# The later adaLN modulation of a streaming Conformer layer: sums over slab rows on ScalarE and GpSimd, turned by transposes, in place of column-group products

## The chip, the cores and the metric

The kernel runs on one core of a Trainium2 chip. A core has five engines with instruction queues of their own: TensorE (PE in the profile, its weight loads PEld), VectorE (DVE), ScalarE (ACT), GpSimd (POOL) and SyncE (SP), which here only issues DMAs. Each engine works through its queue in order and waits on semaphores for the others. TensorE writes to PSUM; GpSimd can work in SBUF only. The metric is the device time of one execution in microseconds, the median of several runs.

## What is computed

One layer of a streaming encoder, for a prompt of 2048 rows and a sample of 64 rows (`T` = 2112 rows in all), width 1024, in float32. The change is in its first lines, the modulation by the conditioning vector `c`:

```python
mod = jax.nn.silu(c) @ p['w_ada'] + p['b_ada']
sh1, sc1, gt1, sh2, sc2, gt2 = [m[:, None, :] for m in jnp.split(mod, 6, axis=-1)]
h = rms_norm(x, p['norm1_g']) * (1 + sc1) + sh1
z = h @ p['w_in']          # convolution pair, q, k, v, two gates
...
x = x + gt1 * (merged @ p['w_o'])
h2 = rms_norm(x, p['norm2_g']) * (1 + sc2) + sh2
gate, up = jnp.split(h2 @ p['w_ffn_in'], 2, axis=-1)
x = x + gt2 * ((jax.nn.silu(gate) * up) @ p['w_ffn_out'])
```

`c` is one row of 1024 for the prompt and one for the sample, `w_ada` is 1024 x 6144. So the modulation is a product of two rows with a matrix of 24 MB, and it gives six vectors of 1024 for each of the two. The first two, `sh1` and `sc1`, are needed at once; `sh2`, `sc2`, `gt1` and `gt2`, the later modulation, are needed only in the second phase, behind the attention.

## The kernel before

**Phases.** The first phase goes over four blocks of rows (`PBLOCKS`, 576 + 3 x 512) and, in each, over the stages of `ORDER`: q, 0, k, 1, v, 2, 3, g. The stages q, k and v are projections (`qkv`), the stages 0 to 3 one quarter each of the convolution input (`glu`), the stage g the 16 tiles of gates. Between the matmuls of these stages run the attention, the convolution and the norms. The second phase, over `CBLOCKS`, has the two mixers' output projections and the FFN. Large products are made of three matmuls, with each operand split into a high and a low float32r part; the split of a weight is a ScalarE copy (`whi`) and a subtraction (`wlo`).

**The order of the work** is written by a planner while the program is built. Every engine is wrapped in a `Meter` (L88), which adds the estimated time of each instruction to that engine's load in `Stream.load` (L183): a matmul of 512 columns 213 ns, a ScalarE pass 220 + 0.83 n ns, a GpSimd operation 60 + 2.25 n ns. After each trio of matmuls `spend` (L212) calls `tick` if 500 ns of planned TensorE time have gone by; it calls the functions that are due and lets each `Lane` make one step or several of its generators (`pump`, L145). A generator yields the planned time from which it may go on, `stream.when(engine)` being the end of that engine's planned load less 200 ns (`LAG`). `PE_LAG` is 400 ns and `TURN_LAG` 2500 ns. `drain` (L166) runs a lane's generators to their ends at once. The matmuls keep the order in which they are written out (`manual_schedule`, L1686); the queues of the other engines are ordered by the compiler's scheduler from data dependences and that order.

**The later modulation.** `MOD_HALVES` (L561) lists its eight halves: for each of the four vectors (`c6` = 3, 4, 2, 5) two halves of 512 columns. A half is four slabs of `w_ada`, each 256 rows x 512 columns as a tile of 128 partitions x 2 x 512 (tag `wmod`, 4 buffers of 512 KB). `Slabs` (L235) loads them through SP's queue: a slab's `done` (L259) makes its buffer free when TensorE has passed, and the next slab's load is issued from there. `mod_steps` (L901) makes one half at the end of each stage in `MODS` (L562): `mod_sums` (L855) multiplies four slabs with the columns of `silu(c)` in `cl`, padded to 32, in four column groups of TensorE at a time (`tile_position`), 16 products a half; `mod_rows` copies the result to SBUF (tile `R`); `mod_columns` (L876), 2.5 us later by the plan, adds the groups up and turns rows into columns by two products with the constant `sel`, and VectorE adds the bias. At the end the gates' vectors are transposed and stored to `gt_d`. 

**Around it.** `attend` (L1551) runs a head of attention: scores (`sc`), maximum on VectorE, exponential on ScalarE, transposes (`ptp`) and the product with v (`po`). `convolve` (L1274) is VectorE's filler: 31 taps a quarter, each `y = u * w + y` over 512 columns in SBUF (`y<-u,wd,y`). `conv_norm` (L1296) has the LayerNorm sums, added up on GpSimd and finished by a product with `ones` (tile `pm`). `temp` (L783) gives one of seven scratch tiles of 128 x 512. `ps_g` has five PSUM banks. From block 2's stage g on the `wmod` buffers serve the attention's q and k (L1445).

Of the kernel before, what the change touches and what calls it, by code (L numbers as in the profile page):

```python
# [8 lines left out]
F32 = mybir.dt.float32  # L9
F32R = mybir.dt.float32r  # L10
AF = mybir.ActivationFunctionType
ALU = mybir.AluOpType
AX = mybir.AxisListType
# [3 lines left out]
P = 128  # L17
D = 1024
KT = 8
# [24 lines left out]
PE_LAG = 400.0  # L44
TURN_LAG = 2500.0
# [513 lines left out]


MOD_HALVES = [(c6, half) for c6 in (3, 4, 2, 5) for half in range(2)]  # L561
MODS = {at: 1 for at in ((1, 0), (1, 1), (1, 2), (1, "g"), (2, 0), (2, 1), (2, 2), (2, 3))}  # L562

ORDER = [(b, st) for b in range(4) for st in ("q", 0, "k", 1, "v", 2, 3, "g")]

# [23 lines left out]
def mod_order():  # L589
    for ct in range(0, KT, 2):  # L590
        yield from (("mod", c6, ct // 2, h, 0) for c6 in (0, 1) for h in range(2))
    yield from (("mod", *half, i) for half in MOD_HALVES for i in range(4))
# [30 lines left out]
def streaming_layer(ctx: ExitStack, tc: tile.TileContext, I, O):  # L623
    nc = tc.nc
    stream = Stream()
    pe, dve, act, gps = (
        Meter(e, n, stream) for e, n in ((nc.tensor, "pe"), (nc.vector, "dve"), (nc.scalar, "act"), (nc.gpsimd, "pool"))
    )
# [28 lines left out]
    ident = const.tile([P, P], F32, name="ident")  # L657
# [8 lines left out]
    A1 = const.tile([P, KT, 2], F32, name="A1")  # L666
    B1 = const.tile([P, KT, 2], F32, name="B1")
    A2 = const.tile([P, KT, 2], F32, name="A2")
    B2 = const.tile([P, KT, 2], F32, name="B2")
    cols = const.tile([P, 76], F32, name="cols")  # L670
    gates_c = const.tile([P, 2, 2, KT], F32, name="gates_c")
# [6 lines left out]
    g1, g2 = cols[:, 0:8], cols[:, 8:16]  # L678
    bdw, lng, lnb = cols[:, 16:20], cols[:, 20:24], cols[:, 24:28]
    b_ada = cols[:, 28:76]  # L680
# [95 lines left out]
    ps_g = p1.enter_context(tc.tile_pool(name="ps_g", bufs=5, space=PSUM))  # L776
    ps_a = p1.enter_context(tc.tile_pool(name="ps_a", bufs=1, space=PSUM))
    wk = p1.enter_context(tc.tile_pool(name="wk", bufs=1))
    cl = wk.tile([P, KT, 32], F32, name="cl")
# [3 lines left out]
    def temp(name, shape=(P, 512)):  # L783
        return wk.tile(list(shape), F32, tag="t", name=name, bufs=NT)
# [70 lines left out]
    def mod_sums(pa, keys):  # L855


        for i, key in enumerate(keys):
            w = M.get(key)
            a, b = w.shape[1:]  # L860
            for j in range(4):

                k, c = divmod(j * 2 * P, b)
                pe.matmul(
                    pa[32 * j : 32 * j + 32], cl[:, a * i + k], w[:, k, c : c + 2 * P], start=i == 0,
                    stop=i == len(keys) - 1, tile_position=(0, 32 * j),
                )
            M.done()

    def mod_rows(pa):  # L870
        R = temp("R", pa.shape)
        stream.after("dve", "pe")
        dve.tensor_copy(R, pa)
        return R

    def mod_columns(pc, R, c6, ct, nh):  # L876


        pc = pc.rearrange("p (e n) -> p e n", e=2)
        for e in range(2):  # L880
            pe.matmul(pc[:, e], R[:, e * P : e * P + P], sel, start=True, stop=True)
        stream.after("dve", "pe")
        pc = pc[:, :, 2 * (nh - 1) : 2 * (2 * nh - 1)].rearrange("p e (h s) -> p e h s", h=nh)
        cs = slice(ct, ct + 2 * nh)

        def place(a):
            return a[:, cs].rearrange("p (h e) s -> p e h s", e=2)

        def wide(a):
            return a.rearrange("p (h e) -> p e h", e=2).unsqueeze(3).to_broadcast([P, 2, nh, 2])  # L890

        bias = wide(b_ada[:, 8 * c6 + ct : 8 * c6 + ct + 2 * nh])
        gates_of = lambda i: gates_c[:, i].rearrange("p s k -> p k s")
        out = place({0: B1, 1: A1, 3: B2, 4: A2}[c6] if c6 not in (2, 5) else gates_of((2, 5).index(c6)))
        dve.tensor_tensor(out, pc, bias, ALU.add)
        if c6 in (1, 4):
            dve.tensor_tensor(out, out, wide({1: g1, 4: g2}[c6][:, cs]), ALU.mult)
        elif c6 in (2, 5):
            dve.tensor_scalar(out, out, {2: 0.25, 5: 0.5}[c6], None, ALU.mult)

    def mod_steps():  # L901
        for c6, half in MOD_HALVES:
            pa = ps_g.tile([P, 512], F32, tag="gp", name="pa")
            mod_sums(pa[:, : 2 * P], [("mod", c6, half, i) for i in range(4)])
            R = mod_rows(pa[:, : 2 * P])
            stream.at(
                stream.when("dve") + TURN_LAG, lambda pa=pa, R=R, c6=c6, half=half: mod_columns(pa[:, 2 * P :], R, c6, 4 * half, 2)
            )
            yield
        stream.flush()  # L910
        pt = ps_g.tile([P, 512], F32, tag="gp", name="pt")
        pe.transpose(pt[:32, :P], gates_c.rearrange("p c s k -> p (c s k)"), ident)
        row = temp("row")
        dve.tensor_copy(row[:32, :P], pt[:32, :P])
        nc.sync.dma_start(gt_d.rearrange("c s (k n) -> (c s k) n", n=P), row[:32, :P])
        yield

    def first_rows():
        places = ((wa, "x", 3), (wa, "x", 3), (wa, "x", 3), (wk, "kk", 1), (wk, "q2", 1))
# [748 lines left out]
    norm_lane, work = Lane({}, wide=NORM_W), Lane({}, wide=5)  # L1668
    attn = Lane(ATTN, ATTN_NS, wide=2, young=True)
    conv, tail = Lane({"dve": CONV_ROOM}, burst=4), Lane({})  # L1670
    stream.lanes = [norm_lane, work, attn, tail, conv]

    hh = wk.tile([P, KT, QB + SMP], F32R, tag="hh", name="hh")
    hl = wk.tile([P, KT, QB + SMP], F32R, tag="hl", name="hl")
# [4 lines left out]
    M = Slabs(nc.sync, nc.scalar, wa, stream, list(mod_order()), source, 4)  # L1679
# [5 lines left out]
    ordered = ExitStack()  # L1685
    ordered.enter_context(tc.manual_schedule(engines={mybir.EngineType.PE}))  # L1686
    norm_lane.add(cached_kv())
    mods = mod_steps()
    norms = {}
    for b, stage in ORDER:  # L1690
        lo, hi = PBLOCKS[b]
        if stage == "q":
            free, ahead = {"columns": 0}, {}
            if b + 1 < len(PBLOCKS):
                ahead = {t: norm_tile(hi, t, free) for t, _ in token_tiles(*PBLOCKS[b + 1])}
        if stage == "q" and b == 0:
            pass
        elif stage in ("q", "k", "v"):
            qkv(b, "qkv".index(stage), norms)
            if stage == "k":  # L1700
                work.wide = 3
            if stage == "v":

                def heads(b=b):
                    work.drain()
                    stream.flush()
                    attention(b)
                    if b == 3:
                        attn.burst, attn.spacing = 2, 0.0

                stream.at(stream.load["pe"] + HEADS_NS, heads)
        elif stage == "g":
            spare["open"] = b >= 2 and ("wide" if b == len(PBLOCKS) - 1 else "narrow")
            for g in gates(b, free):
                if g == SIDE_G - 4 and b == len(PBLOCKS) - 1:
                    spare["open"] = False
                if g == NORM_G:
                    to_load += list(ahead)
                    for _ in range(3):
                        load_ahead()  # L1720
                    for gen in ahead.values():
                        norm_lane.add(gen)
                if g == SIDE_G and b == len(PBLOCKS) - 1:
                    work.drain()
                    conv.drain()
                    while spare["heads"] and now["scored"] < spare["heads"][-1]:
                        attn.push()
                    stream.flush()
                    side.close()
                    wc = ctx.enter_context(tc.tile_pool(name="wc", bufs=1, side="right"))  # L1730
                    cs = tile_chunks(*CBLOCKS[0])[0]
                    src = load_mixed(*cs, 0)
                    first_gates = gate_columns(*cs, 0)
            norms = ahead
        else:
            if b == 0 and stage == 1:
                bias_rows()
            if stage == 0:
                conv.drain()
                tail.drain()  # L1740
                y = wk.tile([P, 4, YW], F32, tag="y", name="y")
            conv.add(convolve(glu(b, stage), y, stage, b))
            if stage == 3:
                if b == 0:
                    tail.add(conv_norm(y, 0, SMP, 0))
                    tail.add(conv_norm(y, SMP + HIST, QB, SMP))
                else:
                    tail.add(conv_norm(y, 0, QB, lo, b == len(PBLOCKS) - 1))
        for _ in range(MODS.get((b, stage), 0)):
            next(mods)  # L1750
    next(mods)
    attn.drain()
    conv.drain()
    tail.drain()
# [6 lines left out]
    ps_g = ctx.enter_context(tc.tile_pool(name="ps_c", bufs=4, space=PSUM))  # L1761
    wk = ctx.enter_context(tc.tile_pool(name="wk2", bufs=1))
    work = Lane({}, 600.0)
# [182 lines left out]
    for s, (lo, hi) in enumerate(CBLOCKS):  # L1946
        tiles = token_tiles(lo, hi)
        half = (hi - lo) // 2
        gt1, groups, hs = {}, [], None
        chunks = tile_chunks(lo, hi)  # L1950
        for i, (c0, c1) in enumerate(chunks):
# [30 lines left out]
            ws = {}  # L1982
# [385 lines left out]
        last = last_rows(s)  # L2368
# [14 lines left out]
        ws = [W.get(("fo", f)) for f in last]  # L2383
# [40 lines left out]
```

## Time and profile before

Three runs took 2940.25, 2942.64 and 2944.25 us, median 2942.64. The profile is of one execution, whose span from the first to the last instruction is 2938.6 us; it gives no other time of that execution.

| Engine | busy us | share of the span | instructions |
|---|---|---|---|
| span | 2938.6 | | 44831 |
| PE | 2887.0 | 98% | 16193 |
| PEld | 2584.9 | 88% | 16193 |
| DVE | 2059.1 | 70% | 3650 |
| ACT | 1362.6 | 46% | 2453 |
| POOL | 1167.1 | 40% | 753 |

All lines of engine work bear L105, the line of the wrapper that records them, so instructions are told apart by their tiles. A row of the timeline has the start in us from the span's start, the duration in us, engine, line, operation, output<-inputs, partitions x elements, the count where several are merged, and in brackets the idle time ahead of it with what ended it. Matmuls overlap in the pipeline: what one costs is the distance from its start to the next one's, not its duration. A row of groups has the count, then the busy time in us and the mean ns of one, then the idle time just before them. A row of the tile view has the shortest, median and longest duration in ns and the first and last start. A row of a table by stretches has from:to and the length, then for each engine the busy us and the number of its instructions, then the granted TensorE clock, the DMA engines' share and GB/s.

### The profile page before, as it was taken

What the parts mean: (1) busy time and instruction counts of PE and PEld (TensorE: products, weight loads), DVE (VectorE), ACT (ScalarE), POOL (GpSimd) and SP (SyncE); (2) the same over time, 40 slices, a digit from 0 to 9 for tenths busy, and PEclk for the clock granted to TensorE, in tenths of its full rate; (3) what the DMA queues carried; (4) which work ended last, traced back from release to release, by engine and by line L of the source; (5) the groups of instructions that cost most, each with busy time, mean ns of one, the idle gap of its engine ahead of it and who ended that gap; (6) DMA issues with size and microseconds to landing.
All of it is one profiled execution on the core that took longest, in us unless ns stands there. A gap on an engine that the chain in (4) does not pass through costs nothing.

```text
span 2938.6 us, 44831 instructions
## 1 busy us (share of the span) xinstructions
PE 2887.0 (98%) x16193; PEld 2584.9 (88%) x16193; DVE 2059.1 (70%) x3650; ACT 1362.6 (46%) x2453; POOL 1167.1 (40%) x753
## 2 busy tenths in 40 slices
PE   7999999999999999999999999999999999999999
PEld 5899777888888888888999998999999999999998
DVE  5897798668967876577777756666667557566666
ACT  3346543661564266563444345444444345444442
POOL 1201310111011003554566452366567742465667
PEclk9999999999999999999999999999999999999999
DMA  9989899978996997984444975333333965333333
GB/s 322 317 296 312 280 291 306 302 243 307 285 294 196 316 269 228 291 299 157 144 144 146 294 260 199 97 122 94 115 115 104 346 220 179 97 103 106 115 107 127
DMA packets 467067, 628.04 MB, mean 214 GB/s; under 512 B 36196, under 2 KB 314584, under 8 KB 466845
## 3 DMA queue, kind: packets, MB, share of 16 engines
q1 hardware_dynamic: 452944, 606.11, 64.1%
q10 hardware_dynamic: 13901, 19.08, 1.9%
q8 instruction: 127, 2.08, 0.3%
q14 instruction: 95, 0.78, 0.1%
HBM read 476.53 MB, written 148.54 MB: 213 GB/s over the span
## 4 chain that ended last, share of the span: by engine, by line
PE 47%; DVE 2%; ACT 1%; issue 1%; DMA 1%; POOL 0%; ACTq 0%; POOLq 0%; DVEq 0%
PE ps L105 28%; PE pd L105 14%; PE pw L105 5%; ACT whi L105 0%; DVE wlo L105 0%; DMA wst<-in_w_ffn_in 0%; DVE pw L105 0%; DVE ps L105 0%; DVE t L105 0%; POOL ws L105 0%; DMA tg<-g_d 0%; DVE acc L105 0%; DVE sums L105 0%; PE pt L105 0%; ACT xn L105 0%
## 5 line engine op out<-in xcount | busy, mean ns | idle before, releaser
L105 PE MATMUL ps<-t,whi 128*128 128x384 f32 (+1 forms) x2112 | 501.9, 322 | 2.7 <-ACT u L105 0.8
L105 POOL TENSOR_TENSOR wlo<-wst,whi 128x1024 fp32r<-128x1024 f32 (+1 forms) x159 | 364.1, 2302 | 215.3 <-ACT whi L105 215.2
L105 ACT ACTIVATE whi<-wst 128x1024 fp32r<-128x1024 f32 (+1 forms) x265 | 258.3, 979 | 318.8 <-PE ps L105 134.9
L105 PE MATMUL ps<-b,whi 128*128 128x384 f32 (+1 forms) x1584 | 380.4, 325 | 6.5 <-DVE v L105 2.1
L105 PEld LDWEIGHTS ps<-t,whi 128*128 128x128 f32 x2112 | 367.7, 188 | 10.2 <-ACT u L105 3.4
L105 DVE SCALAR_TENSOR_TENSOR y<-u,wd,y 128x512 f32<-128x512 f32 (+1 forms) x480 | 370.0, 774 | 8.2
L105 PE MATMUL ps<-hh,whi 128*128 128x512 f32 (+2 forms) x992 | 362.0, 365 | 0.1
L105 DVE TENSOR_TENSOR acc<-acc,pd 128x512 f32<-128x512 f32 x482 | 322.2, 685 | 47.9 <-PE pd L105 45.3
L105 PE MATMUL ps<-hh,wlo 128*128 128x512 f32 (+2 forms) x992 | 344.6, 347 | 0.0
L105 PE MATMUL ps<-hl,whi 128*128 128x512 f32 (+2 forms) x992 | 344.0, 347 | 0.0
L105 PE MATMUL ps<-t,wlo 128*128 128x384 f32 (+1 forms) x1056 | 338.2, 321 | 0.0
L105 PE MATMUL pd<-whi,hid 128*128 128x512 f32 x912 | 297.4, 391 | 0.5 <-DVE hid L105 0.3
L105 PEld LDWEIGHTS ps<-b,whi 128*128 128x128 f32 x1584 | 276.8, 188 | 14.8 <-DVE v L105 3.2
L105 ACT ACTIVATE pr<-pr,sm 128x640 f32<-128x640 f32 (+3 forms) x272 | 202.2, 749 | 133.3 <-DVE sm L105 130.9
L105 PE MATMUL ps<-b,wlo 128*128 128x384 f32 (+1 forms) x792 | 256.0, 323 | 0.0
L105 POOL TENSOR_TENSOR r<-t,mhalf 128x1 f32<-128x1 f32 (+2 forms) x68 | 82.8, 1225 | 408.0 <-DVE t L105 355.1
L105 DVE TENSOR_TENSOR wlo<-wst,whi 128x1024 fp32r<-128x1024 f32 (+1 forms) x106 | 135.3, 1280 | 101.6 <-ACT whi L105 100.1
L105 PEld LDWEIGHTS ps<-hh,wlo 128*128 128x128 f32 x992 | 186.3, 188 | 22.7
L105 PEld LDWEIGHTS pd<-whi,hid 128*128 128x128 f32 x912 | 171.1, 188 | 36.9 <-DVE acc L105 1.2
L105 PEld LDWEIGHTS ps<-hh,whi 128*128 128x128 f32 x992 | 186.7, 188 | 17.7 <-issue 2.5
L105 PEld LDWEIGHTS ps<-hl,whi 128*128 128x128 f32 x992 | 187.1, 189 | 14.7 <-issue 1.7
L105 PEld LDWEIGHTS ps<-t,wlo 128*128 128x128 f32 x1056 | 198.1, 188 | 0.8
(233 smaller groups left out, 6309.7 us busy)
## 6 DMA issues: line engine op xcount, KB each, us to landing
whi<-w_din_h SPq DMA_DIRECT2D x72, 512.0 KB, 6.8
wlo<-w_din_l SPq DMA_DIRECT2D x72, 512.0 KB, 6.9
wst<-sum_d SPq DMA_DIRECT2D x131, 256.0 KB, 2.9
wfo<-in_w_ffn_out SPq DMA_DIRECT2D x64, 512.0 KB, 4.0
wmod<-in_w_ada SPq DMA_DIRECT2D x46, 512.0 KB, 9.1
sum_d<-ws SPq DMA_DIRECT2D x88, 256.0 KB, 2.3
wst<-in_w_ffn_in SPq DMA_DIRECT2D x85, 256.0 KB, 3.2
wst<-in_w_in SPq DMA_DIRECT2D x40, 512.0 KB, 6.1
```

Of the source, the lines that this page charges most:

```text
L105: self.last = f(*args, **kw)
```

## The change

The eight halves are no longer multiplied on TensorE. For each of the eight groups of 128 rows in a half (`k`), ScalarE scales the slab's rows by `silu(c)` of the prompt into a scratch tile and by `silu(c)` of the sample in place, each partition with its own factor. GpSimd adds these up over `k`, the sums standing in the first slab's own buffer. What remains is a sum over 128 partitions: TensorE transposes the two sums of 128 x 512 in four squares each, and VectorE adds each square up along its rows (`tensor_reduce`), which gives the columns that the bias, scale and factor are applied to as before. All four slabs are released together at the end of a half.

The halves are generators in a lane of their own, the last in the list. Half i is added at the end of stage `MODS[i]`, beginning one entry earlier than before, at (0,"g") instead of (1,0); ahead of each addition the lane is drained, and once more at (2,3). `mod_columns` keeps the cases of the first two vectors only; `sel`, `cl` and `mod_sums` stay for these.

```diff
-MODS = {at: 1 for at in ((1, 0), (1, 1), (1, 2), (1, "g"), (2, 0), (2, 1), (2, 2), (2, 3))}
+MODS = [(0, "g"), (1, 0), (1, 1), (1, 2), (1, "g"), (2, 0), (2, 1), (2, 2)]
...
+    def mod_sum(c6, half, last):
+        ws = [M.get(("mod", c6, half, i)) for i in range(4)]
+        first = temp("first")
+        accs = [ws[0][:, 1], ws[0][:, 0]]
+        for k in range(KT):
+            w = ws[k // 2][:, k % 2]
+            t = temp("term") if k else first
+            act.activation(t, w, AF.Copy, scale=cl[:, k, 0:1])
+            act.activation(w, w, AF.Copy, scale=cl[:, k, 1:2])
+            if k:
+                stream.after("pool", "act")
+                gps.tensor_tensor(accs[1], accs[1], w, ALU.add)
+                gps.tensor_tensor(accs[0], first if k == 1 else accs[0], t, ALU.add)
+            yield stream.when("pool")
+        yield stream.when("pool") + PE_LAG
+        total = wk.tile([P, 2, 4], F32, tag="total", name="total", bufs=2)
+        for s in range(2):
+            pt = ps_g.tile([P, 4, P], F32, tag="gp", name="pt")
+            for j in range(4):
+                pe.transpose(pt[:, j], accs[s][:, j * P : j * P + P], ident)
+            stream.after("dve", "pe")
+            dve.tensor_reduce(total[:, s], pt, AX.X, ALU.add)
+        for _ in ws:
+            M.done()
...
+        dve.tensor_tensor(out, total, wide(b_ada[:, 8 * c6 + 4 * half : 8 * c6 + 4 * half + 4]), ALU.add)
+        if c6 == 4:
+            dve.tensor_tensor(out, out, wide(g2[:, cs]), ALU.mult)
         elif c6 in (2, 5):
             dve.tensor_scalar(out, out, {2: 0.25, 5: 0.5}[c6], None, ALU.mult)
-
-    def mod_steps():
-        for c6, half in MOD_HALVES:
-            pa = ps_g.tile([P, 512], F32, tag="gp", name="pa")
-            mod_sums(pa[:, : 2 * P], [("mod", c6, half, i) for i in range(4)])
-            R = mod_rows(pa[:, : 2 * P])
-            stream.at(
-                stream.when("dve") + TURN_LAG, lambda pa=pa, R=R, c6=c6, half=half: mod_columns(pa[:, 2 * P :], R, c6, 4 * half, 2)
-            )
-            yield
-        stream.flush()
+        if not last:
+            return
+        yield stream.when("dve") + PE_LAG
         pt = ps_g.tile([P, 512], F32, tag="gp", name="pt")
         pe.transpose(pt[:32, :P], gates_c.rearrange("p c s k -> p (c s k)"), ident)
...
-    stream.lanes = [norm_lane, work, attn, tail, conv]
+    mods = Lane({})
+    stream.lanes = [norm_lane, work, attn, tail, conv, mods]
...
-        for _ in range(MODS.get((b, stage), 0)):
-            next(mods)
-    next(mods)
+        if (b, stage) in MODS:
+            mods.drain()
+            i = MODS.index((b, stage))
+            mods.add(mod_sum(*MOD_HALVES[i], i + 1 == len(MODS)))
+        elif (b, stage) == (2, 3):
+            mods.drain()
```

More of the change, by code (lines that the diff above doesn't have):

```diff
@@ L892, in mod_columns @@
         bias = wide(b_ada[:, 8 * c6 + ct : 8 * c6 + ct + 2 * nh])
-        gates_of = lambda i: gates_c[:, i].rearrange("p s k -> p k s")
-        out = place({0: B1, 1: A1, 3: B2, 4: A2}[c6] if c6 not in (2, 5) else gates_of((2, 5).index(c6)))
+        out = place((B1, A1)[c6])
         dve.tensor_tensor(out, pc, bias, ALU.add)
-        if c6 in (1, 4):
-            dve.tensor_tensor(out, out, wide({1: g1, 4: g2}[c6][:, cs]), ALU.mult)
+        if c6:
+            dve.tensor_tensor(out, out, wide(g1[:, cs]), ALU.mult)
@@ new lines, in mod_sum @@
+    def mod_sum(c6, half, last):
[22 more added lines that the diff above has]
+            M.done()
+        cs = slice(4 * half, 4 * half + 4)
+        wide = lambda a: a.unsqueeze(1).to_broadcast([P, 2, 4])
+        if c6 in (2, 5):
+            out = gates_c[:, (2, 5).index(c6), :, cs]
+        else:
+            out = {3: B2, 4: A2}[c6][:, cs].rearrange("p k s -> p s k")
+        dve.tensor_tensor(out, total, wide(b_ada[:, 8 * c6 + 4 * half : 8 * c6 + 4 * half + 4]), ALU.add)
+        if c6 == 4:
+            dve.tensor_tensor(out, out, wide(g2[:, cs]), ALU.mult)
@@ L915, in mod_steps @@
         nc.sync.dma_start(gt_d.rearrange("c s (k n) -> (c s k) n", n=P), row[:32, :P])
-        yield
     def first_rows():
@@ L1687, in streaming_layer @@
     norm_lane.add(cached_kv())
-    mods = mod_steps()
     norms = {}
```

## The prediction

> **What bounds the kernel now.** I read the page's busy shares first, then its chain, then TensorE's timeline around the work that goes.
>
> ```profile
> PE 2887.0 (98%) x16193; PEld 2584.9 (88%) x16193; DVE 2059.1 (70%) x3650; ACT 1362.6 (46%) x2453; POOL 1167.1 (40%) x753
> PE 47%; DVE 2%; ACT 1%; issue 1%; DMA 1%; POOL 0%; ACTq 0%; POOLq 0%; DVEq 0%
> ```
>
> TensorE (PE) is busy 98% and the chain is nearly all PE. So a microsecond taken off PE's own list counts, and so does any wait put into it: PE's order is fixed by the planner, and what stands behind a waiting instruction waits too. The spare time of the other engines is worth something only where PE needn't wait for them.
>
> **PE's part.** The later products are 8 halves of 32 records (tile view, from 200 us on; first and last start are in the row); a half costs what PE's start-to-start times show:
>
> ```profile
> L105 PE MATMUL pa<-wmod,cl x256: 379/379/404, 356.6 to 747.9; 128*32 128x256 f32 x128
> ```
> ```profile
> 731.72 1.93 PE L105 MATMUL pa<-wmod,cl 128*32 128x256 f32 x32
> 733.58 0.50 PE L105 MATMUL ps<-hh,whi 128*128 128x512 f32 x1
> 733.92 0.40 PE L105 MATMUL ps<-hl,whi 128*128 128x512 f32 x1
> 734.15 0.39 PE L105 MATMUL ps<-hh,wlo 128*128 128x512 f32 x1
> ...
> 737.11 0.60 PE L105 MATMUL pa<-sel,R 128*128 128x128 f32 x4
> 737.47 0.48 PE L105 MATMUL ps<-hh,whi 128*128 128x512 f32 x1
> ```
> ```profile
> 618.22 0.60 PE L105 MATMUL pt<-ident,x_t 128*128 128x128 f32 x4
> 618.57 0.47 PE L105 MATMUL ps<-whi,hh 128*128 128x512 f32 x1
> 618.88 0.39 PE L105 MATMUL ps<-wlo,hh 128*128 128x512 f32 x1
> ```
>
> Products: 733.58 - 731.72 = 1.86, and the next matmul takes 0.34 instead of 0.23: 1.97 us. The two products with `sel`: 737.47 - 737.11 = 0.36, and about 0.09 behind them. Removed: 8 x 2.42 = 19.4 us. Added are 8 transposes a half; four take 618.57 - 618.22 = 0.35, with 0.08 behind a group: 8 x 0.78 = 6.2 us. PE's list gets 13.2 us shorter. The gates' last transpose is in both.
>
> **What is added elsewhere**, by the nearest forms (mean ns behind the busy time):
>
> ```profile
> L105 ACT ACTIVATE junk<-x_t 128x512 f32<-128x512 f32 x24 | 14.9, 623 | 3.1 <-DMA x_t<-in_x_prompt 3.0
> L105 POOL TENSOR_TENSOR s<-s,ln 128x512 f32<-128x512 f32 x12 | 15.9, 1324 | 32.3 <-ACT ln L105 32.2
> L105 DVE TENSOR_REDUCE ssq<-sq 128x8 f32<-128x512 f32 x32 | 21.6, 678 | 8.0 <-ACT sq L105 7.8
> ```
>
> A half is 16 ScalarE passes (16 x 0.62 = 10.0 us), 14 GpSimd adds in one dependent row (14 x 1.32 = 18.5 us) and two reductions (1.4 us; a 0.42 us copy goes). Eight halves: 80 us ScalarE, 148 us GpSimd. As busy time that disappears, both engines being under half full. What matters is the 20 us from a half's first pass to its last add, where that must be over, and whom it holds up.
>
> **The last half.** Where the stages end:
>
> ```profile
> 313.15 0.39 PE L105 MATMUL ps<-whi,hh 128*128 128x512 f32 x1
> ```
> ```profile
> 454.36 1.93 PE L105 MATMUL pa<-wmod,cl 128*32 128x256 f32 x32
> ```
> ```profile
> 696.53 1.93 PE L105 MATMUL pa<-wmod,cl 128*32 128x256 f32 x32
> ```
> ```profile
> 746.36 1.93 PE L105 MATMUL pa<-wmod,cl 128*32 128x256 f32 x32
> ```
>
> A half now starts where its predecessor's products stood (the first at the end of (0,"g"), 313) and must be over at the next entry. The last starts at the end of (2,2), 731.72, and is drained at (2,3), 746.36: 14.6 us for a row that takes 20. Its slabs aren't there at once either. The planner spaces a step by two passes (2 x 645 ns), two adds (2 x 1212) less 400 of lags, and the next tick: some 3.6 us, so 27 us for a half, 29 in PE's real time (planned 213 ns a matmul, 228 in the rows). Half 6, from 696.5, thus ends near 726, and only then are the last four slabs asked for:
>
> ```profile
> 734.42 2.11 SPq L249 DMA_DIRECT2D wmod<-in_w_ada  x4
> ```
> ```profile
> 365.80 2.28 SPq L249 DMA_DIRECT2D wmod<-in_w_ada  x4
> ```
> ```profile
> wmod<-in_w_ada SPq DMA_DIRECT2D x46, 512.0 KB, 9.1
> ```
>
> SP reaches them 2.7 us (734.42 after 731.72) to 9.2 us (365.80 after 356.6) behind the matmuls that free them, and they take 9.1 to land: about 738. Two passes and 14 adds later it is 758; PE has stood since 746.4, 11.5 us. Then the gates' transpose waits for reductions, bias and scale on DVE, behind a convolution tap or two: 2.5 us. Low bound, slabs there at 731.7: 5 + 1 = 6 us. High bound, each add taking turns with a tap (next part): 14 x (1.32 + 0.67) = 28, so 767, 21 + 3 = 24 us. I take 15, near the first working. Nothing covers this: everything PE has next stands behind it.
>
> The transposes of the other seven halves are placed 0.4 us behind the planned last add. The nearest case, the LayerNorm sums that wait for GpSimd with the same lag, hardly waits:
>
> ```profile
> PE pm L105 <- DVE h L105: 0.4, 1, 0.4
> ```
>
> Between 0 and 2 us each; I take 0.4, 3 us in all.
>
> **DVE against GpSimd.** Both read SBUF. Overlaps in the timelines, GpSimd rows first:
>
> ```profile
> 545.26 4.85 POOL L105 TENSOR_TENSOR y<-y,s 128x512 f32<-128x512 f32 x4 [13.44 <-DVE sm L105]
> ```
> ```profile
> 547.45 1.71 DVE L105 TENSOR_SCALAR y<-y,cols 128x512 f32<-128x512 f32 x1 [1.65 <-ACT ln L105]
> 549.19 1.46 DVE L105 SCALAR_TENSOR_TENSOR ln<-ln,y 128x512 f32<-128x512 f32 x1
> ```
> ```profile
> 1164.19 8.00 POOL L105 TENSOR_TENSOR wlo<-wst,whi 128x1024 fp32r<-128x1024 f32 x3 [11.07 <-ACT whi L105]
> ```
> ```profile
> 1164.66 5.29 DVE L105 TENSOR_TENSOR part_l<-ln,part_h 128x512 fp32r<-128x512 f32 x2 [0.51 <-ACT part_h L105]
> ```
> ```profile
> L105 DVE SCALAR_TENSOR_TENSOR y<-u,wd,y 128x512 f32<-128x512 f32 x360 | 268.6, 750 | 6.3
> ```
>
> Two subtractions that take about 0.7 us elsewhere took 5.29 beside three long GpSimd ones: the engines took turns. The 1.46 stands against 0.75 for the same operation, the form of the taps. And the taps fill the stages in which the halves run (all engines, then the taps alone):
>
> ```profile
> 411.00:454.00 43.00, 43.00 (x233) 34.63 (x225) 33.17 (x69) 14.93 (x35) 1.45 (x3) 1.00 0.91 308
> ...
> 659.00:697.00 38.00, 38.00 (x210) 30.30 (x211) 31.53 (x52) 7.57 (x14) 8.58 (x6) 1.00 0.81 265
> 697.00:732.00 35.00, 35.00 (x184) 28.23 (x180) 26.55 (x41) 3.54 (x6) 1.45 (x3) 1.00 0.94 331
> 732.00:746.00 14.00, 14.00 (x91) 11.28 (x84) 13.64 (x25) 2.56 (x5) 0.21 (x1) 1.00 1.01 376
> ```
> ```profile
> 411.00:454.00 43.00, 22.98 (x31) 1.00 0.91 308
> ...
> 697.00:732.00 35.00, 23.08 (x31) 1.00 0.94 331
> ```
>
> DVE (third pair) has 43 - 33.2 = 9.8, 6.5 and 8.4 us to spare there. If every add shuts a tap out for its whole length, a half costs DVE 18.5 us, and 9 to 12 of them are more than it has; five halves (those from 357, 411, 454, 659, 697) run beside taps: 5 x 10 = 50 us, the upper end. The lower end is 0: taps are filler, and between 659 and 732 PE hardly depends on DVE (ScalarE busy 7.6 and 3.5 us there, so next to no softmax, and five PSUM banks stand between PE and its readers). I take 8, from the two earlier halves with attention beside them, nearer to 0.
>
> By the Trainium skill, page "SBUF — State Buffer", section "Who interferes with whom", a DVE instruction with two SBUF inputs and a GpSimd instruction that reads SBUF exclude each other for the whole instruction. This speaks against the change; taken literally it gives the upper end. The trace agrees for the long additions above and differs for the small powers, during which five taps ran on at their usual 0.67 apart:
>
> ```profile
> 670.22 2.05 POOL L105 TENSOR_TENSOR r<-t,mhalf 128x8 f32<-128x8 f32 x1 [9.09 <-DVE t L105]
> ```
> ```profile
> 670.02 3.90 DVE L105 SCALAR_TENSOR_TENSOR y<-u,wd,y 128x512 f32<-128x512 f32 x5
> ```
>
> **Slabs that land late** hold up ScalarE's queue: behind its first pass stand exponentials and PSUM copies that PE needs. A half that ends close to the next one's start leaves nothing for the 12 to 18 us from freeing to landing. That can be so at 357 (half 0 shares GpSimd with the LayerNorm) and 454: 0 to 15 us; I take 3, as planned ends near 343 and 441 leave 13.
>
> **Sum**: -13.2 + 15 + 3 + 8 + 3 = +15.8 us on the span of 2938.6, 2954.4. The runs' median lies 4.0 above that span: 2958.4 us.
>
> **Rivals and chances.** What can't be told from no change is 0.2%, 5.9 us.
> - Forecast, 0.42: PE's gain is given back at (2,3) and a little by DVE. 2950 to 2970.
> - DVE becomes the bound, 0.18: adds and taps exclude each other in full. For it: the 5.29 us row. Against: filler can wait. -13.2 + 22 + 30 (of 50) + 3 = +42: 2984.
> - ScalarE blocked by late slabs, 0.10: -13.2 + 15 + 3 + 8 + 15 = +28: 2970.
> - The gain stays, 0.20 (other side): half 6 ends early, the last slabs are in place at 731.7 and the row runs unhindered, so the wait at (2,3) is at its low bound; it decides below 7 us there with nothing elsewhere. -13.2 + 6 = -7: 2935, at best 2929.
> - It cancels, 0.10: 13 us at (2,3), nothing else: 2942.
>
> Slower 0.70, same 0.10, faster 0.20. The range 2935 to 2988 leaves out the better half of the fourth case and the worst of the second; the forecast's own is 2950 to 2970.
>
> **What would show it.** PE idle in one piece of 10 us or more near 746, released by GpSimd and then by DVE, with the last `wmod` loads landing near 738; PE busy 13 us less; taps above 1 us beside adds, their mean above 750 ns; in other halves less than 1 us of waiting ahead of the transposes. I am wrong if that one wait is under 7 us, or if PE's waits for `sm`, `pl` and `kn` grow by over 20 us between 357 and 500.

## The result and the profile after

The changed kernel takes 3013.3 us (median of four runs, 3009.6 to 3015.7) against 2941.4 (four runs, 2940.2 to 2944.3): ratio 1.0245, 95% interval 1.0230 to 1.0259. It is 72 us slower, where 16 were predicted. All times here are of fast runs; one of e11 (4578.9 us) and one of the kernel before (5781.7 us), far slower than all others, are left out. The profiled execution has a span of 3007.6 us. First the page's busy shares and its chain:

```profile
PE 2895.7 (96%) x15969; PEld 2593.6 (86%) x15969; DVE 2132.2 (71%) x3658; ACT 1439.8 (48%) x2581; POOL 1334.9 (44%) x865
PE 48%; ACT 1%; DVE 1%; DMA 0%; issue 0%; POOL 0%; ACTq 0%; DVEq 0%
```

PE has 224 matmuls fewer, as planned, but is busy 8.7 us longer, and stands still 3007.6 - 2895.7 = 111.9 us against 51.6. Together that is 69 us, the growth of the span. The table by stretches, after and then before, says where (the same times, not quite the same work, since the changed kernel is already behind):

```profile
400.00:500.00 100.00, 79.10 (x340) 63.05 (x339) 83.91 (x138) 47.91 (x98) 44.03 (x34) 0.87 0.73 244
...
700.00:800.00 100.00, 80.21 (x363) 65.52 (x361) 96.20 (x116) 41.25 (x69) 62.92 (x45) 0.92 0.71 255
```
```profile
400.00:500.00 100.00, 98.58 (x535) 80.46 (x535) 81.60 (x162) 37.75 (x79) 5.88 (x8) 1.00 0.93 303
...
700.00:800.00 100.00, 100.00 (x537) 82.42 (x536) 87.07 (x154) 34.90 (x61) 4.81 (x8) 1.00 0.92 298
```

Where the halves meet the convolution, PE's share falls from 99 and 100 to 79 and 80, its granted clock from 1.00 to 0.87 and 0.92, and DVE is busy 96% of the second stretch. PE's waits, after (total us, times, longest):

```profile
PE pt L105 <- POOL wmod L105: 25.1, 3, 17.3
PE sc L105 <- DVE sm L105: 14.8, 8, 4.7
PE pt L105 <- DVE kn L105: 7.9, 3, 5.2
PE po L105 <- issue: 6.5, 1, 6.5
```

Only the first was a wait that the prediction had priced by itself. The group of the taps of 512 columns, whose mean was 750 ns before, and then one of the `sm` waits in PE's, DVE's and GpSimd's timelines:

```profile
L105 DVE SCALAR_TENSOR_TENSOR y<-u,wd,y 128x512 f32<-128x512 f32 x360 | 310.5, 866 | 6.6
```
```profile
453.07 0.39 PE L105 MATMUL ps<-hh,wlo 128*128 128x512 f32 x1
458.13 1.22 PE L105 MATMUL sc<-kk,q 128*128 128x512 f32 x2 [4.67 <-DVE sm L105]
459.15 0.63 PE L105 MATMUL ps<-hh,whi 128*128 128x512 f32 x1
459.57 0.63 PE L105 MATMUL ps<-hl,whi 128*128 128x512 f32 x1
```
```profile
452.62 4.98 DVE L105 SCALAR_TENSOR_TENSOR y<-u,wd,y 128x512 f32<-128x512 f32 x3
457.52 0.55 DVE L105 CUSTOM_DVE_ANT_0 pr<-sc,bias 128x384 f32<-128x384 f32 x1
458.00 0.08 DVE L105 DVE_READ_ACCUMULATOR2_ANT sm<- 128x1 f32 x1
```
```profile
450.27 1.74 POOL L105 TENSOR_TENSOR wmod<-wmod,term 128x512 f32<-128x512 f32 x1
451.98 1.74 POOL L105 TENSOR_TENSOR wmod<-wmod 128x512 f32<-128x512 f32 x1
453.68 3.37 POOL L105 TENSOR_TENSOR wmod<-wmod,term 128x512 f32<-128x512 f32 x2
```

Three taps take 4.98 us, about as long as the three adds beside them. In the kernel before, three in a row take 2.33:

```profile
680.88 2.33 DVE L105 SCALAR_TENSOR_TENSOR y<-u,wd,y 128x512 f32<-128x512 f32 x3
```

Behind the three taps in DVE's queue stands the maximum (`sm`) that frees a bank for the next scores, and PE's fixed order stands behind those scores for 4.67 us. Then matmuls of 512 columns follow each other by 459.57 - 459.15 = 0.42 us and not 0.23, for some microseconds: the granted clock is 0.50 from 458 to 462. That is the second part of the price.

The last half stands where it was predicted:

```profile
787.47 0.39 PE L105 MATMUL ps<-hh,wlo 128*128 128x512 f32 x1
805.20 2.34 PE L105 MATMUL pt<-ident,wmod 128*128 128x128 f32 x8 [17.34 <-POOL wmod L105]
808.72 0.39 PE L105 MATMUL pt<-ident,gates_c 128*32 128x128 f32 x1 [1.19 <-DVE gates_c L105]
```
```profile
L249 SPq DMA_DIRECT2D wmod<-in_w_ada x8: 373/443/793, 703.0 to 780.0; - x8
```
```profile
776.21 1.30 POOL L105 TENSOR_TENSOR wmod<-first,term 128x512 f32<-128x512 f32 x1
...
787.34 3.32 POOL L105 TENSOR_TENSOR wmod<-wmod,term 128x512 f32<-128x512 f32 x2 [9.48 <-ACT term L105]
...
805.11 1.26 POOL L105 TENSOR_TENSOR wmod<-wmod 128x512 f32<-128x512 f32 x1
```

SP asks for the last slab at 780.0 (the last start in the tile view's row, from 700 to 900 us). GpSimd waits 9.48 us for passes, and most of the rest of the row runs beside taps. Those passes also stand in ScalarE's queue behind an exponential that waits for VectorE until 785.6; whether that or the slabs held them isn't settled. PE stands 17.3 + 1.2 us.

### The profile page after: what moved, and what is told of

Its sections match the earlier page's. It is cut to its first block, busy times and chain, and to the rows that moved or that the text cites. A ratio compares the mean times of both kernels' runs of the same rounds, so it can differ in the third digit from the quotient of the medians.

```text
span 3007.6 us, 44749 instructions
## 1 busy us (share of the span) xinstructions
PE 2895.7 (96%) x15969; PEld 2593.6 (86%) x15969; DVE 2132.2 (71%) x3658; ACT 1439.8 (48%) x2581; POOL 1334.9 (44%) x865
## 4 chain that ended last, share of the span: by engine, by line
PE 48%; ACT 1%; DVE 1%; DMA 0%; issue 0%; POOL 0%; ACTq 0%; DVEq 0%
PE ps L105 29%; PE pd L105 14%; PE pw L105 4%; DVE wlo L105 1%; ACT whi L105 0%; DMA cin<-o_d 0%; ACT xn L105 0%; DMA tg<-g_d 0%; DVE ps L105 0%; PE pt L105 0%; ACT t L105 0%; DVE hid L105 0%; ACT hid L105 0%; DVE t L105 0%; ACT u L105 0%
## 5 line engine op out<-in xcount | busy, mean ns | idle before, releaser
L105 DVE SCALAR_TENSOR_TENSOR y<-u,wd,y 128x512 f32<-128x512 f32 (+1 forms) x480 | 411.8, 861 | 8.4
```

The costliest lines, as they stand in the source:

```text
L105: self.last = f(*args, **kw)
```

## The experiments

All are the changed kernel with the edit shown. Each was timed against the kernel before on its own chip (2940.5 to 2942.5 us), and the ratio is to that. "PE idle" is the profiled span less PE's busy time. Five of the sixteen times lie in a range that was expected (that of e3, theory A of e7, theory B of e9, e11 and e12); the others lie between or outside the ranges given for them, so it is their differences that are read below.

| Run | What | us | ratio, 95% | PE idle | DVE busy |
|---|---|---|---|---|---|
| after | the change | 3013.3 | 1.0230 to 1.0259 | 111.9 | 2132.2 |
| e1 | no adds | 2958.3 | 1.0028 to 1.0077 | 68.5 | 2071.1 |
| e2 | transposes don't wait | 3004.0 | 1.0180 to 1.0239 | 103.4 | 2137.2 |
| e3 | memsets for adds | 2958.3 | 1.0030 to 1.0088 | 71.1 | 2072.6 |
| e4 | no ScalarE passes | 3021.9 | 1.0238 to 1.0303 | 120.4 | 2129.7 |
| e5 | neither passes nor adds | 2947.9 | 1.0011 to 1.0036 | 68.7 | 2066.4 |
| e6 | copies for adds | 2968.8 | 1.0083 to 1.0117 | 77.2 | 2089.6 |
| e7 | one entry earlier | 3000.8 | 1.0188 to 1.0227 | 105.2 | 2134.0 |
| e8 | halves 27 us apart | 3064.0 | 1.0408 to 1.0442 | 159.9 | 2093.4 |
| e9 | halves 40 us apart | 3001.7 | 1.0196 to 1.0231 | 101.4 | 2108.1 |
| e10 | sums on VectorE | 2969.6 | 1.0075 to 1.0108 | 81.1 | 2138.6 |
| e11 | the same, in e9's places | 2962.2 | 1.0060 to 1.0094 | 72.4 | 2144.5 |
| e12 | planner told of the turns | 3000.9 | 1.0190 to 1.0224 | 103.9 | 2116.4 |
| e13 | e12, one entry earlier | 3011.7 | 1.0228 to 1.0265 | 108.4 | 2135.0 |
| e14 | VectorE's sums, planner not told | 2985.6 | 1.0140 to 1.0173 | 92.1 | 2144.3 |
| e15 | e10, earlier, gates' row later | 2957.6 | 1.0043 to 1.0073 | 68.9 | 2132.7 |
| e16 | e15 without its sums | 2958.1 | 1.0042 to 1.0076 | 77.2 | 2064.9 |

**Which part costs (e1 to e5).** TensorE's order is that of the change in all five.

```diff
 # e1: the planner is charged, nothing is added
-                gps.tensor_tensor(accs[1], accs[1], w, ALU.add)
-                gps.tensor_tensor(accs[0], first if k == 1 else accs[0], t, ALU.add)
+                for _ in range(2):
+                    stream.add("pool", "tensor_tensor", 512, (), {})
```

> Leaves out the 112 GpSimd adds; the planner still counts them, so TensorE's order is that of the change, and ScalarE's passes and the transposes stay. If GpSimd is the cause (its row of adds that the transposes wait for, and its hold on the SBUF port against VectorE's taps): 2925 to 2945 us, taps back to a mean of 750 ns, gaps of TensorE between 300 and 900 us under 15 us in all. If the planner's new order or ScalarE's passes are the cause: 2975 us or more.

```diff
 # e2
-                pe.transpose(pt[:, j], accs[s][:, j * P : j * P + P], ident)
+                pe.transpose(pt[:, j], ident, ident)
```

> Adds and passes stay, but the transposes read the constant identity and not the sums, so TensorE never waits for GpSimd directly (the outputs' modulation is wrong). If the wait for the row of adds is the cause: below 2955 us. If VectorE's delay by the port is the greater part: 2970 to 2990 us, with the waits for sm, kn and pl and the tap mean of 860 ns unchanged.

```diff
 # e3: as e1, and in the adds' place
+                for dst in (w, accs[1], t, accs[0]):
+                    nc.gpsimd.memset(dst, 0.0)
```

> Each pair of adds becomes four GpSimd memsets of the same tiles: the same dependences, GpSimd busy for a like time, but it reads no SBUF (the sums are zero). If GpSimd's reads shut out VectorE's two-input instructions: taps near 750 ns, VectorE busy some 40 us less than with the change, 2940 to 2975 us, what is above 2935 being the direct waits. If GpSimd's busy time or its dependences as such are the cause: within 12 us of 3013.

```diff
 # e4: the planner is charged; the adds take the raw slabs
-            act.activation(t, w, AF.Copy, scale=cl[:, k, 0:1])
-            act.activation(w, w, AF.Copy, scale=cl[:, k, 1:2])
+            for _ in range(2):
+                stream.add("act", "activation", 512, (), {})
```

> Leaves out the 128 ScalarE passes (the raw slab rows are added); the planner still counts them, the adds and transposes stay. If ScalarE's passes hold up exponentials and copies: below 2985 us. If GpSimd is the cause: 2995 to 3015 us, a few us less since the adds can start one pass earlier.

e5 has the edits of e1 and of e4 together.

> The ScalarE passes and the GpSimd adds are both left out, so the later modulation is the transposed raw slab; the planner is charged as if they were there, and TensorE's order, the slabs' loads, the transposes and the reductions are those of the change. Against the run without adds (2958, 16 us above before although TensorE's list is 13 shorter) only the 128 ScalarE passes go. Theory A, the passes stand in ScalarE's queue ahead of copies and exponentials that TensorE needs: the 6.4 us wait for `po` near 467 goes and the time falls to 2930 to 2945. Theory B, the slabs' and weights' order on SP and the planner's order of the rest make the 16 us: 2952 to 2962, with the waits for `whi` (w_dqkv) and for gates_c still there.

Without the adds 55.1 us go (3013.3 to 2958.3). With memsets in their place, which keep GpSimd's queue, its waits for ScalarE and the transposes' dependence on it, the same 55.1 go. The groups of e3, the taps and the memsets:

```profile
L105 DVE SCALAR_TENSOR_TENSOR y<-u,wd,y 128x512 f32<-128x512 f32 x360 | 269.8, 753 | 6.5
```
```profile
L914 POOL MEMSET wmod<- 128x512 f32 x168 | 87.0, 541 | 54.6 <-ACT wmod L105 49.1 <-issue 2.2
```

The taps are back at 753 ns, and the table by stretches gives PE 88 and 95 in place of 79 and 80:

```profile
400.00:500.00 100.00, 88.13 (x421) 72.11 (x420) 78.49 (x150) 54.97 (x106) 32.61 (x65) 0.95 0.88 280
700.00:800.00 100.00, 94.56 (x456) 79.48 (x455) 86.44 (x147) 46.20 (x80) 31.47 (x61) 0.97 0.91 298
```

The memsets are shorter than the adds (four take 2.2 us, two adds 3.0), so GpSimd's time isn't quite the same, and in e3 PE never waits for them. But e1 and e3 agree, so the memsets' 113 us of GpSimd's time cost nothing by themselves. What costs is that the adds read SBUF, and that their row is long.

e2 separates these two. It takes away only TensorE's waits for the sums, all 25.1 us of them, and gets 9.4 us. The other 45.7 (3004.0 in e2 to 2958.3 in e1; e2 has two runs, 1.5 us apart) are what the adds cost beside those waits. The waits of e2:

```profile
PE sc L105 <- DVE sm L105: 19.3, 11, 4.6
PE pt L105 <- DVE gates_c L105: 11.2, 1, 11.2
PE po L105 <- issue: 6.5, 1, 6.5
```

VectorE is late at (2,3) too, and now it is waited for.

What the passes cost isn't shown. By the medians e1 is 10.4 us above e5, but the two intervals overlap, and in the profiled executions, 2.7 us apart, PE stands 68.5 and 68.7 us. e4, with adds and without passes, is 8.6 us slower than the change. It is no clean test either: with no pass to wait for, the first half's adds run from 60 to 81 us, where the change has them from 326 to 363, others follow each other more closely, and the waits for `sm` and `kn` are 63 us where the change has 23. One place where the passes stand ahead of something can be seen in e1, in ScalarE's timeline:

```profile
469.01 0.83 ACT L105 ACTIVATE pr<-pr,sm 128x640 f32<-128x640 f32 x1 [0.61 <-DVE sm L105]
469.74 0.71 ACT L105 ACTIVATE first<-wmod,cl 128x512 f32<-128x512 f32 x1
470.35 0.71 ACT L105 ACTIVATE term<-wmod,cl 128x512 f32<-128x512 f32 x1
470.96 1.32 ACT L105 ACTIVATE wmod<-wmod,cl 128x512 f32<-128x512 f32 x2
472.30 0.59 ACT L105 ACTIVATE other<-po 64x512 f32<-64x512 f32 x1
```

Four passes (2.6 us) stand ahead of the copy that frees a PSUM bank of `po`, in a wait of PE of 6.4 us (it is the `po` row in the waits of the change). With neither passes nor adds (e5) that gap is gone, and still the kernel is 6.6 us above before, though its list is shorter.

**How much of it is reading (e6).**

```diff
 # e6: as e1, and in the adds' place
+                nc.gpsimd.tensor_copy(accs[1], w)
+                nc.gpsimd.tensor_copy(accs[0], t)
```

> Each pair of GpSimd adds is replaced by two GpSimd copies with the same destinations (so the sums are left out), with the planner charged as before: the queue, the waits and the destinations stay, but an instruction reads one SBUF operand and not two. Theory A, GpSimd's reads shut VectorE's two-input instructions out for as long as a GpSimd instruction lasts, however many operands it reads: VectorE's busy time rises with GpSimd's added time, some 20 to 60 us above the 2072 of the run without adds, and the time lies at 2975 to 3010. Theory B, only GpSimd instructions with two SBUF operands do it: VectorE busy 2070 to 2080 and 2955 to 2962, as with the memsets.

Between the two theories: 2968.8, with VectorE busy 17 us more than in e3. A copy lasts half as long as an add and delays a tap less: taps beside copies take 0.96 us, beside adds 1.45, beside memsets 0.75, and elsewhere 0.76 (means over the taps of 512 columns between 150 and 900 us; "beside" is an overlap of 0.3 us or more). Reading one operand is enough. Whether the add costs more because it reads two or because it lasts longer isn't separated.

**Other places for the halves (e7 to e9).** The entries of `MODS` and of the last drain:

```diff
-MODS = [(0, "g"), (1, 0), (1, 1), (1, 2), (1, "g"), (2, 0), (2, 1), (2, 2)]
+# e7, drained at (2, 3)
+MODS = [(0, 3), (0, "g"), (1, 0), (1, 1), (1, 2), (1, "g"), (2, 0), (2, 1)]
+# e8, drained at (2, 1); (b, "g", g) is gate g of block b
+MODS = [(0, "g", 8), (0, "g", 11), (0, "g"), (1, "g", 5), (1, "g", 8), (1, "g", 11), (1, "g"), (2, "q")]
+# e9, drained at (2, 1)
+MODS = [(0, "g", 7), (0, "g"), (1, 0), (1, 2), (1, "g", 4), (1, "g", 9), (1, "g", 13), (2, "q")]
```

> The change with every half begun one entry of the list earlier and the last drain still at (2,3), so the last half has two stages (36 us) in place of one. Theory A, VectorE runs behind through the taps whatever the last half does, and its own waits take the place of the 17 us wait as they did when the transposes didn't wait for the sums: 3000 to 3012. Theory B, the wait for the last sums is a cost by itself and comes off in full with the half clock behind it: 2985 to 2995.

> The change with its halves begun in the stages in which no convolution taps run: at the gates 8 and 11 and the end of (0,g), the gates 5, 8 and 11 and the end of (1,g), and the end of (2,q), the last drained at (2,1). Theory A, the loss comes from taps and adds taking turns: VectorE's busy time is within 15 us of the 2071 without adds, GpSimd's adds take about 1.3 us, and the time is 2930 to 2950, near or under the kernel before. Theory B, a half costs TensorE about the same wherever it runs (ScalarE's passes, the slabs' loads, the waits ahead of the transposes): 2975 to 3010.

> The change with its halves begun 40 us or more apart, five of the eight where no convolution taps run: gate 7 and the end of (0,g), the ends of (1,0) and (1,2), gates 4, 9 and 13 of (1,g), the end of (2,q), the last drained at (2,1). The run with halves 27 us apart (3064) drained each half some 12 us before its sums were there (85 us of waits on the sums), but its VectorE was busy 2093, not 2132. Theory A, both costs are real, the row that is drained too early and the taps that take turns with adds: waits on the sums under 25 us in all, VectorE busy 2085 to 2105, time 2945 to 2970. Theory B, a half costs TensorE its 10 us of wait wherever it is put: 2990 or more.

e7 has no long wait for the last sums any more and gives back 12.5 us, while PE's waits for `sm` rise to 27.5. e8 keeps VectorE nearly free of turns with taps (busy 2093) and is the slowest of all: with its slabs' loads a half needs 40 us and more there, and the drains, about 27 us apart by the plan, put PE behind the sums:

```profile
PE pt L105 <- POOL wmod L105: 85.1, 13, 16.8
```

e9 was meant to have neither cost and missed its 2945 to 2970 by 32 us. The waits on the sums are 23.4 (85.1 in e8), and VectorE is busy 37 us more than in e1 where the change has 61, yet `sm` (16.6) and `pl` (8.6) stay. Only 19 of the 37 us are the taps': GpSimd reads SBUF while other VectorE work runs there too, the LayerNorm's for instance, so a place without taps isn't a place without turns.

**Another engine, and the planner's knowledge (e10 to e14).** In e10 VectorE makes the sums, with no passes and no adds:

```diff
 # e10
+            if k == 0:
+                dve.tensor_scalar(first, w, cl[:, k, 0:1], None, ALU.mult)
+                dve.tensor_scalar(w, w, cl[:, k, 1:2], None, ALU.mult)
+            else:
+                dve.scalar_tensor_tensor(accs[1], w, cl[:, k, 1:2], accs[1], ALU.mult, ALU.add)
+                dve.scalar_tensor_tensor(accs[0], w, cl[:, k, 0:1], first if k == 1 else accs[0], ALU.mult, ALU.add)
 # e12, behind the change's two adds; e13 adds the MODS of e7
+                stream.load["dve"] = max(stream.load["dve"], stream.load["pe"]) + 1100
 # e14: as e10, but written with nc.vector past the planner, which is charged
 # the passes and adds of the change
```

> The sums are made by VectorE alone, w*c + sum in one instruction (128 of them, no ScalarE passes and no GpSimd adds), in the places of the change. VectorE gets some 128 x 0.75 = 96 us of its own work, where the change gave it 61 us by turn-taking. Theory A, what VectorE loses in these stages is what TensorE loses, whether its own work or turns cost it: 3000 to 3030. Theory B, VectorE's work there can be put off and only an engine held still in the middle of an instruction hurts, and a half's row is 12 us long, not 20: 2945 to 2965.

> VectorE's sums in the places of the spaced run, five halves where no taps run and VectorE has more time to spare. Theory A: 2930 to 2950, under the change everywhere and near the kernel before, since only three halves meet taps (3 x 12 us of VectorE's time) and TensorE's list is 13 shorter. Theory B, the row's place doesn't matter: as the run with VectorE's sums in the change's places, within 8 us.

> The change, with the planner charged 550 ns of VectorE for each GpSimd add (61 us of longer VectorE work over 112 adds). Theory A, VectorE's lost time costs TensorE because the planner doesn't know of it and writes taps ahead of the maxima and copies that TensorE waits for: with the charge VectorE's waits for `sm`, `pl`, `kn` fall and the time is 2970 to 2990. Theory B, an instruction held in the middle delays VectorE whatever the plan says: 3000 to 3015.

> The same charge, with the halves begun one entry earlier, so the last half has two stages. Theory A: 12 us below the run with the charge alone (what the earlier entry was worth without it: 3013 to 3001), 2958 to 2978. Theory B: as the earlier entry alone, 2995 to 3005.

> VectorE's own sums in the places of the change, but written past the planner, which is charged the ScalarE passes and GpSimd adds of the change: TensorE's order is that of the change, and only where VectorE's 96 us were known (2969.6 with them known) differs. Theory A, unplanned VectorE time is what costs: 2990 to 3030, with waits for `sm` and `pl`. Theory B, only an instruction that is held in the middle costs: 2962 to 2975.

VectorE does all the work itself and is busy only 6 us longer than in the change (2138.6 against 2132.2):

```profile
L105 DVE SCALAR_TENSOR_TENSOR wmod<-wmod,cl 128x512 f32<-128x512 f32 x104 | 75.3, 751 | 1.9 <-DMA wmod<-in_w_ada 1.9
```

Yet e10 is 44 us faster than the change, and e14, in which TensorE has the very order of the change, 28. GpSimd's help takes from VectorE nearly as much time as the work itself would: 61 us of turns (the change less e1, 0.55 for each of 112 adds) against 72 (e10 less e5, 0.75 for a w*c + sum, which needs no pass either). e14 is 16 us slower than e10, with waits for `sm` of 18.8 against 3.8. Its planner doesn't know of VectorE's sums and plans for passes and adds that aren't there, so time on VectorE that the plan doesn't hold seems to be part of the price. But telling the planner in the change itself gives only 12 us (e12), and e13 loses 11 of them again: theory A is borne out by neither. Nor is it settled why a microsecond of turns costs more (46 us of time for 66 of VectorE, e2 less e1) than one of unplanned sums (38 for 78, e14 less e5). e11 has the same sums in e9's places and is within 8 us of e10: for VectorE's own sums the place matters little.

**What is left of the saving (e15, e16).** e15 is e10 with the `MODS` of e7 and the gates' last transpose in a generator of its own behind (2,3), so that the drain doesn't hold it; e16 leaves the sums out and charges the planner nothing for them.

> VectorE's sums, known to the planner, the halves one entry earlier and the gates' transpose left to its own time behind (2,3). In the run with VectorE's sums TensorE stood 12.6 + 1.2 us for the last half, with 17.1 us at half clock behind it. Theory A, these are all that keeps it above before: 2969.6 - 13.8 - 8.5 = 2947, 2940 to 2952. Theory B, VectorE is as late elsewhere when the last half isn't: 2958 to 2970.

> The passes and adds are left out and the planner isn't charged for them, the halves begin one entry earlier, and the gates' transpose is left to its own time behind (2,3). TensorE's list is that of the change. Theory A, the list's 13 us are real and the run without passes and adds gave them back in waits that the charged order and the drain at (2,3) brought (5.4 us for gates_c with half clock behind it): 2927 to 2937, the kernel's median less 13 within some us. Theory B, the transposes cost TensorE as much as the products did, or any change of order costs some 10 us: 2941 to 2950.

e15 took off 12 us, not 22, and doesn't reach before. It is as fast as e16, which leaves the sums out and has an order of its own. That order alone keeps e16 16.8 us above before, without any sums, passes or adds, as e5's keeps it 6.6 above, so e15 has more to pay for than its sums. The page row of e16 and the largest of its waits:

```profile
PE 2879.2 (97%) x15969; PEld 2584.5 (87%) x15969; DVE 2064.9 (70%) x3658; ACT 1363.1 (46%) x2453; POOL 1168.2 (40%) x753
```
```profile
PE ps L105 <- DMA wlo<-w_dqkv_l: 9.2, 3, 7.3
PE sc L105 <- DVE sm L105: 8.1, 6, 4.0
```

PE's busy time is 7.8 us below before, so its list did get shorter. But it stands 77.2 us against 51.6, for a weight that landed late, for `sm`, for others in small pieces, and it is at half clock for 44 us of the execution where before has 14. The list itself is 12.4 us shorter (19.4 - 8 x 0.88): from the first start to that of the next matmul, eight transposes take 0.79 us in e5, and 0.09 behind them, where the prediction had 0.78 in all. So two plans without the added work (e5, e16) cost about 19 and 29 us beside their list. In e5, 5.4 of that is the wait for `gates_c` at the last drain; which of the shifted transfers and copies makes the rest isn't settled.

## Why the prediction was wrong

The sign was right, though for another main reason than the one forecast; the size wasn't. Put together from the runs: list, new order and passes +16.0 (e1 less before), the waits for the sums +9.4 (the change less e2), the adds beside those waits +45.7 (e2 less e1): 71.1 of the measured 71.9. The prediction had -10.2 for the first (-13.2, and 3 for late slabs), 18 for the second (15 and 3) and 8 for the third.

- **PE's list, -13.2**: there, as 12.4 (224 matmuls fewer, PE's busy time down 5.6 and 7.8 in e5 and e16 in spite of more half clock). What failed is what the sum left out: that a shorter list is a new plan for every queue, here about 19 to 29 us.
- **The last half, 15**: right in place and size (17.3 + 1.2). It is worth less than it lasts, 9 to 12 us (e2, e7), because VectorE is late there as well.
- **The other halves, 3**: 7.8, nearly all of it one wait of 7.6 at the end of (1,0), where half 0 is drained before its row is done. From its first pass to its last add a half took 27 to 52 us, where the prediction had 29; the other drains came late enough for that.
- **DVE against GpSimd, 8 of 0 to 50**: this is the step that failed, a term that was mis-sized. It measured 46 (e2 less e1), near its upper end, and that is 38 of the 56 us by which the sum was off. The prediction took a value near the lower end because taps are filler. They are filler for the planner; for VectorE's queue they are instructions ahead of others, and a maximum behind three long taps is late whatever the taps are for. "PE hardly depends on DVE" was read from ScalarE's small share between 659 and 732, but the losses at `sm`, `kn` and `pl` begin near 400. By the Trainium skill, page "SBUF — State Buffer", section "Who interferes with whom", a VectorE instruction with two SBUF inputs contends with GpSimd instructions that read SBUF and not with those that only write it: e3 and e6 bear out both halves. The small powers, the row on which the prediction leaned against that rule, read 8 elements a partition; they say nothing of an add of 512. (The five taps beside them follow each other by 0.79 us, (3.90 - 0.75) / 4, the usual distance of taps in a row, and not by 0.67 as the prediction says.)
- **Late slabs, 3**: ScalarE's waits for a slab come to 0.9 us in the change. The passes stand ahead of a copy in one place (2.6 us of a wait of 6.4); what they cost in all isn't shown.
- **The half clock** was in no step: the change has 85 us of it, before 14. PE's busy time is 8.7 up with a list 12.4 down, so it costs some 21 us by this estimate, spread over the terms above.

Of the rivals "DVE becomes the bound" named the mechanism and priced it at +42. Its 30 for the turns should have been 46, its 22 for the last half 9, and its -13.2 for the list +16 with order and passes. Of the signs to look for, PE idle in one piece and the long taps came as said; PE busy 13 us less didn't, and one wait ahead of the transposes was 7.6 and not under 1. The waits for `sm`, `pl` and `kn` grew by 4 us between 357 and 500 (7.1 to 11.0) and by 15 over the whole execution, under the 20 that were to be the alarm, because the delay stands under other names and in the clock too.

## What to carry to other kernels

An engine that is half idle isn't free if its instructions read SBUF while VectorE runs two-input instructions: charge VectorE for each of them (0.55 us for an add of 512 columns here), and first compare with doing the work on VectorE itself. In queues that run in order there is no filler at run time: ask what stands behind each instruction that gets longer. And where the order is planned as a whole, try the edit once with its work left out, which shows what the new order alone costs.

## What the runs showed of the hardware

- Beside adds, taps of 512 columns take 1.45 us for 0.76, `kn<-kn,r` 1.34 for 0.68, and a product with one SBUF tensor as input, `y<-u,wd,cols`, 1.34 for 0.54 (5 of them against 3). Instructions that read PSUM (`pl<-ptp,ph` 0.69 for 0.69, the reductions of the transposes 0.68 for 0.69) aren't touched. The adds pay too: 1.58 us in the median and 1.26 at the shortest. The turns are shorter than whole instructions: the three taps and three adds above take 1.66 us a pair, where 0.75 and 1.26 one behind the other would be 2.01.
- In the change all ten stands of TensorE of 2.5 us or more (after the first 100 us) were followed by a granted clock of 0.50, for 3 to 8 us after its work had resumed; of four of 1.9 to 2.5 us, two were. The Trainium skill, page "TensorE: Matmul & The Clock Gate", section "What's actually happening", has the clock halved after an idle window of about 3.4 us; here the wait of 2.5 us at `po` near 520 did it as well.
- A ScalarE pass with a factor for each partition takes 712 ns, where the form that the prediction took them for has 623. The Trainium skill, page "ScalarE: Activation LUTs", section "What ACT_TABLE_LOAD costs", gives about 93 ns for such an operand, and the rows agree (89).
